# A mixture-of-experts backbone on one core: weights laid out in blocks by the host, two experts given 64 float32 slots in place of 128 split ones, and another order of the experts

## The chip, the core and the metric

The kernel runs on one core of one Trainium2 chip. The metric is the device time of one execution in microseconds (us), lower is better. Engines are named as the profile names them: PE is the tensor engine (PEld its loads of stationary operands), DVE the vector engine, ACT the scalar engine, POOL the general-purpose engine, SP the engine whose queue issues the loads of weights.

## What is computed

The reference is a two-layer backbone over 256 latent and 256 context tokens of width 1024, in float32. Each layer has a token mixer (attention, retention and pooling heads between one input and one output projection), then a channel mixer: dense SwiGLU in the first layer, the two best of eight expert SwiGLUs in the second. Norms are modulated by a conditioning vector through a large matrix `w_mod`. The part that matters here is the last:

```python
def moe_swiglu(h, router, w1, w3, w2):
    logits = (h @ router).astype(jnp.float32)
    top_vals, top_idx = lax.top_k(logits, TOP_K)
    top_w = jax.nn.softmax(top_vals, axis=-1)
    gates = jnp.sum(jax.nn.one_hot(top_idx, N_EXPERTS, dtype=jnp.float32) * top_w[..., None], axis=-2)
    out = jnp.zeros_like(h)
    for e in range(N_EXPERTS):
        out = out + gates[..., e:e + 1].astype(h.dtype) * swiglu(h, w1[e], w3[e], w2[e])
    return out
```

256 tokens with two experts each make 512 places for eight experts. With the inputs that are timed the experts 0 to 7 get 15, 154, 50, 25, 52, 46, 80 and 90 tokens. Each expert has three matrices of 1024 by 2816 (or 2816 by 1024) float32 numbers, 33 MiB in all, so the eight hold 264 MiB.

## The kernel before

The program is one straight line of instructions for each engine; only the order in which the expert weights are fetched, and a loop at the very end, depend on the data. Weights come through SP's queue in loads of 1 MiB, one `[128, 2048]` float32 tile each (`wload`), into a ring of buffers that is used in turn. In the expert part the ring has 13 buffers (4 of `ring`, 3 of `ring2`, 6 of `ring3`), and one early load goes to memory that is lent (`LENT`). A load is issued when the reader of the load 13 places earlier is done with its buffer, and SP issues loads in order.

Before the change the weight matrices lie in DRAM as the reference has them. A block of rows and columns is picked by the load's pattern, so each partition's 2048 numbers come in pieces as wide as the block: 256 columns (1 KB), 512 (2 KB, `moe_w1` and `moe_w3`), 1024 (4 KB, `moe_w2`), or all 2048 (8 KB, most of `w_mod`).

**Experts** (`experts`). Expert 0 runs first, its address being known at once. The seven others follow by falling load; place 1 is the fullest of them. `SLOTS` has the number of token slots of each place and `RUNS` the order of the places, a pair in one bracket being worked chunk by chunk together. Tokens that find no slot go through the loop at the end. A place of 160 slots is a group of 128 and one of 32. For each place:

- `gather` picks the tokens of the slots by a product with a 0/1 matrix P and modulates them, on PE, then DVE and ACT.
- `up` makes the products with w1 and w3 for 512 features at a time, in five chunks and a half one: 22 loads.
- `act` makes silu(h1) * h3 and turns it by PE transposes (L1251).
- `down` makes the product with w2: 11 loads.
- `combine` weighs the result by the gates (ys, on ACT and then DVE), sends it back to the tokens by 8 products (L1352), and adds it to the sums `macc`.

A group of 128 slots works with split operands: each half load of weights (a unit of 1024 numbers a partition) is split by `wsplit` into a high part `wh` on ACT (L155) and a low part `wl` on DVE (L156), and PE makes three products for each pair of operands (`mm3`, L231 to L233). The pairs wh, wl live in `hl` buffers, four of each in the expert part. A group of 64 or 32 slots uses the float32 weights straight from the ring, in column tiles that work side by side (L1284 up, L1315 down); ACT and DVE have nothing to split for it. Its gathered tokens and its activations are in a tile `few64` (or `few32`), of which there was one.

```python
if m < 128:
    c = max(128, n * m // 128)
    for k in range(k0, k0 + nk):
        for j in range(n // c):
            nc.tensor.matmul(h[i][m * j:m * j + m, :c], lhsT=x[0][:, k],
                             rhs=t[:, k - k0, j * c:j * c + c], start=k == 0, stop=k == KB - 1,
                             tile_position=(0, m * j))
    continue
```

The tokens of the next run are gathered between the chunks of the one that runs (`ready`). Order on each engine follows the program, so what stands behind a waiting instruction on the same engine waits too. `hold` keeps the splits of the first expert's weights behind the routing.

Of the kernel before, what the change touches and what calls it, by code (L numbers as in the profile page):

```python
# [20 lines left out]
D = 1024  # L21
KB = 8
# [7 lines left out]
# One token tile is 128 rows; tiles 0, 1 hold the latent stream, tiles 2, 3 the context.  # L30
# Slots that an expert has in the order in which the experts run: expert 0 runs first, the others
# follow by falling load. What doesn't fit goes through the loop at the end.
SLOTS = (128, 160, 128, 128, 128, 64, 64, 64)
# Which of them run together, chunk by chunk.
RUNS = ((0,), (2,), (3,), (4,), (7,), (1, 6), (5,))
SCRATCH = 4096              # bytes a partition for the descriptors of Pool's DMAs
# [4 lines left out]
# Memory that the experts need late holds some of their first blocks of weights.  # L41
LENT = {11: "few64"}
# [4 lines left out]
def shape_constants():  # L47
    """Tables that follow from the shapes alone."""
# [32 lines left out]
def weave(main, side, ratio):  # L81
    """The steps of main, with `ratio` steps of side after each."""
    due = 0.0
    for _ in main:
        due += ratio
        while due >= 1:
            due -= 1
            next(side, None)


class Net:
# [61 lines left out]
    def split(self, hi, lo, x):  # L153
        """hi + lo == x exactly, each of them a float32r."""
# [3 lines left out]
    def wload(self, src, a, n):  # L158
        """A [128, a, n] block of weights (a * n == 2048) on its way from DRAM."""
        tag = self.lent.pop(0) if self.lent else None  # L160
        if tag:
            t = self.work.tile([128, 2048], F32, name="w", tag=tag, bufs=MA if tag == "acts" else 1)
        else:
            r = self.rings[self.turn % len(self.rings)]
            self.turn += 1
            t = r.tile([128, 2048], F32, name="w", tag="w")
        v = t.rearrange("p (a n) -> p a n", a=a)
        self.nc.sync.dma_start(v, src)
        return v
# [13 lines left out]
    def block(self, src, n, k):  # L183
        """Rows of src from block k on, 2048 elements a partition."""
        a = 2048 // n
        return self.wload(src[k * 128:(k + a) * 128].rearrange("(a p) n -> p a n", p=128), a, n)
# [16 lines left out]
    def product(self, units, outs, op, tail):  # L203
        """op for all units and outputs; the last `tail` units go output by output."""
# [23 lines left out]
    def mm3(self, out, a, b, start, stop):  # L228
        """out += a.T @ b of split operands."""
# [5 lines left out]
    def spin(self, p, n, w):  # L235
        """Products that nobody needs. They keep the PE at its full clock while it waits."""
# [4 lines left out]
    def setup(self):  # L241
# [29 lines left out]
        # silu of both conditioning vectors, as stationary columns  # L271
# [12 lines left out]
        # norm gains and pool scales by feature  # L284
# [14 lines left out]
    def decays(self):  # L299
        """log_sigmoid of the decay logits, on every partition: [layer, direction, head]."""  # L300
# [30 lines left out]
    def mod_group(self, l, g, ms=(), split=0):  # L331
        """2048 columns of c @ w_mod + b_mod, in steps of 128 rows of w_mod: row 32 j + m of the result holds
        512 of them (m: stream, context). In the first `split` steps VectorE weighs the rows for each m of ms
        and sums them by partition, and the tensor engine only sums the partitions."""
# [18 lines left out]
        for k in range(KB):  # L353
            w = self.wload(I["w_mod"][l, k * 128:(k + 1) * 128, g * 2048:(g + 1) * 2048]
                           .rearrange("p (a n) -> p a n", a=1), 1, 2048)
# [53 lines left out]
    def fill(self, n=1):  # L409
        """The next n steps of the modulation that is still to be done."""  # L410
# [3 lines left out]
    def gate_tile(self, l, g, m):  # L414
        """gate * norm_post on every partition."""
# [1212 lines left out]
```

## Time and profile before

| | |
|---|---|
| time of three runs | 1592.82 us median (1589.38 to 1595.25) |
| span of the profiled execution | 1588.2 us; no other time of that one execution is listed, and the three runs lie 1.2 to 7.1 us above its span |
| busy share PE, DVE, ACT, POOL | 97%, 63%, 48%, 2% |
| moved by DMA | 400.09 MB, 252 GB/s in the mean |
| expert part | from the first expert's first product at 806.18 us to the end |

Times are microseconds from the start of the span. A row of the timeline has the start, the length, engine, source line, operation, tiles and the number of instructions merged in it; in square brackets the idle time before it and who ended that. A busy PE is not a PE at its peak, because overlapping products all count as busy; how fast it works is read from the distance between the starts of its products.

### The profile page before, as it was taken

The page shows a single profiled execution, that of the slowest core. Times are in us where ns is not written, and L with a number is a line of the kernel's source. Part 1 is how long each engine was busy: PE and PEld are TensorE (multiplying, and loading weights), DVE is VectorE, ACT ScalarE, POOL GpSimd, SP SyncE. Part 2 cuts the span into 40 slices and gives each one's busy share as a digit, 9 for nine tenths or more (in the row PEclk, how much of TensorE's full clock was granted, in tenths as well). Part 3 has the DMA queues.
Part 4 walks back from the last instruction along what each step waited for, and adds up shares of the span by engine and source line. Part 5 has one row for each costly group of instructions (what it writes and reads, how often), then busy time and mean ns, then how long its engine had stood idle before and what let it go on. Part 6 is the DMA issues. An engine that isn't in the chain of part 4 may idle for free. (4 is left out here: it accounts for less than half of the span.)

```text
span 1588.2 us, 23352 instructions
## 1 busy us (share of the span) xinstructions
PE 1545.9 (97%) x9104; PEld 1167.4 (74%) x9105; DVE 1008.1 (63%) x1712; ACT 761.9 (48%) x1134; POOL 34.1 (2%) x69
## 2 busy tenths in 40 slices
PE   7999999999999999999999999999999999999996
PEld 5776668888888888786678788888887657674562
DVE  3596678764455456886789899999984144443411
ACT  4436644423213223567568878778773133333211
POOL 1010200000000010000000000000000000000000
PEclk9999999999999999999999999999999999999998
DMA  9873313344355533633588999999999999998994
GB/s 313 296 288 106 135 58 117 117 165 161 127 196 189 186 120 107 215 107 133 199 293 326 359 327 344 355 351 355 325 355 327 396 386 382 333 347 309 336 369 169
DMA packets 185574, 400.09 MB, mean 252 GB/s; under 512 B 9060, under 2 KB 60968, under 8 KB 180336
## 3 DMA queue, kind: packets, MB, share of 16 engines
q1 hardware_dynamic: 180432, 392.19, 69.6%
q0 software_dynamic: 2624, 5.54, 1.1%
q8 instruction: 73, 1.20, 0.3%
q10 hardware_dynamic: 2400, 0.79, 0.2%
q14 instruction: 45, 0.37, 0.1%
HBM read 397.41 MB, written 1.08 MB: 251 GB/s over the span
## 5 line engine op out<-in xcount | busy, mean ns | idle before, releaser
L155 ACT ACTIVATE wh<-w 128x1024 fp32r<-128x1024 f32 x442 | 462.0, 1061 | 361.7 <-PE at L233 108.9
L156 DVE TENSOR_TENSOR wl<-w,wh 128x1024 fp32r<-128x1024 f32 x442 | 531.5, 1222 | 158.1 <-ACT wh L155 146.1
L1284 PE MATMUL mm<-w,few 128*64 128x256 f32 (+2 forms) x1856 | 151.1, 335 | 0.0
L1284 PEld LDWEIGHTS mm<-w,few 128*64 128x64 f32 (+1 forms) x1856 | 99.3, 128 | 45.6 <-issue 11.7
L231 PE MATMUL mm<-hh,wh 128*128 128x512 f32 (+1 forms) x256 | 95.7, 374 | 1.2 <-ACT hh L155 1.2
L232 PE MATMUL mm<-hl,wh 128*128 128x512 f32 (+1 forms) x256 | 95.6, 374 | 0.0
L233 PE MATMUL mm<-hh,wl 128*128 128x512 f32 (+1 forms) x256 | 95.3, 372 | 0.0
L231 PE MATMUL mm<-wh,xh 128*128 128x512 f32 (+1 forms) x240 | 93.0, 387 | 0.6 <-ACT xh L155 0.6
L231 PE MATMUL at<-wh,xh 128*128 128x512 f32 (+1 forms) x240 | 90.8, 378 | 0.0
L232 PE MATMUL mm<-wl,xh 128*128 128x512 f32 (+1 forms) x240 | 89.9, 375 | 0.0
L233 PE MATMUL mm<-wh,xl 128*128 128x512 f32 (+1 forms) x240 | 89.7, 374 | 0.0
L232 PE MATMUL at<-wl,xh 128*128 128x512 f32 (+1 forms) x240 | 89.4, 373 | 0.0
L233 PE MATMUL at<-wh,xl 128*128 128x512 f32 (+1 forms) x240 | 89.1, 371 | 0.0
L233 PE MATMUL mm<-wh,hl 128*128 128x256 f32 (+1 forms) x240 | 80.6, 341 | 0.0
L361 DVE SCALAR_TENSOR_TENSOR wsum<-w,sc,wsum 128x1024 f32<-128x1024 f32 x48 | 59.6, 1280 | 30.3 <-DMA w<-in_w_mod_dram 30.3
L1315 PE MATMUL mm<-w,few 128*64 128x512 f32 (+1 forms) x352 | 77.1, 599 | 0.0
L232 PE MATMUL mm<-wl,hh 128*128 128x256 f32 (+1 forms) x224 | 75.3, 339 | 1.8 <-DVE wl L156 1.8
L231 PE MATMUL mm<-wh,hh 128*128 128x256 f32 (+1 forms) x224 | 74.9, 339 | 0.0
L232 PE MATMUL at<-hl,wh 128*128 128x512 f32 (+1 forms) x192 | 71.3, 371 | 0.0
L233 PE MATMUL at<-hh,wl 128*128 128x512 f32 (+1 forms) x192 | 71.3, 371 | 0.0
L231 PE MATMUL at<-hh,wh 128*128 128x512 f32 (+1 forms) x192 | 71.2, 371 | 0.0
L1247 ACT ACTIVATE mg<-mm 128x512 f32<-128x512 f32 (+3 forms) x54 | 24.8, 459 | 68.6 <-PE mm L1284 65.7
(459 smaller groups left out, 2860.6 us busy)
## 6 DMA issues: line engine op xcount, KB each, us to landing
w<-in_moe_w_dram SPq DMA_DIRECT2D x264, 1024.0 KB, 7.1
w<-in_w_mod_dram SPq DMA_DIRECT2D x48, 1024.0 KB, 5.2
w<-in_ffn_w_dram SPq DMA_DIRECT2D x33, 1024.0 KB, 5.5
w<-in_w_in_dram SPq DMA_DIRECT2D x16, 1024.0 KB, 5.2
w<-in_w_out_dram SPq DMA_DIRECT2D x8, 1024.0 KB, 5.2
gate<-gscr POOLq DMA_DIRECT2D x5, 512.0 KB, 4.8
band<-in_band_dram SPq DMA_DIRECT2D x4, 512.0 KB, 7.7
xin<-in_x_dram SPq DMA_DIRECT2D x2, 512.0 KB, 4.0
```

Source lines behind the costliest of these rows:

```text
L155: self.nc.scalar.activation(hi, x, AF.Copy)
L156: self.nc.vector.tensor_sub(lo, x, hi.bitcast(F32))
L231: mm(out, lhsT=a[0], rhs=b[0], start=start, stop=False)
L232: mm(out, lhsT=a[0], rhs=b[1], start=False, stop=False)
L233: mm(out, lhsT=a[1], rhs=b[0], start=False, stop=stop)
L361: nc.vector.scalar_tensor_tensor(x, y, c, x, op0=OP.mult, op1=OP.add)
L1247: nc.scalar.activation(s1[:r, :c], h1[:r, :c], AF.Silu)
L1284: nc.tensor.matmul(h[i][m * j:m * j + m, :c], lhsT=x[0][:, k], rhs=t[:, k - k0, j * c:j * c + c], start=k == 0, stop=k == KB - 1, tile_pos ...
L1315: nc.tensor.matmul(y[0][r:r + m], lhsT=x[0][:, b], rhs=w[:, j, c], start=f + j < a, stop=f + j >= FB - a, tile_position=(0, r))
```

## The change

1. **Layout.** `packed` and `blocks` cut every weight matrix on the host into the blocks that are loaded, so that a load is one contiguous MiB with 8 KB for each partition. `wload` takes that block; its callers give block numbers in place of slices. What lands in SBUF is the same.
2. **Slots.** Place 0 (expert 0) and place 4 (the fourth by load of the others) get 64 slots in place of 128.
3. **Order.** Places run as 0, 2, 4, 3, 5, (1, 6), 7 in place of 0, 2, 3, 4, 7, (1, 6), 5: groups of 64 and of 128 slots alternate.
4. **Memory.** There are two `few64` tiles in place of one, three pairs of `hl` buffers in the expert part in place of four, and no lent memory.

All else of the diff takes comments away, which moves line numbers by some 8 to 15.

```diff
-SLOTS = (128, 160, 128, 128, 128, 64, 64, 64)
-# Which of them run together, chunk by chunk.
-RUNS = ((0,), (2,), (3,), (4,), (7,), (1, 6), (5,))
+SLOTS = (64, 160, 128, 128, 64, 64, 64, 64)
+
+RUNS = ((0,), (2,), (4,), (3,), (5,), (1, 6), (7,))
...
-LENT = {11: "few64"}
...
     def wload(self, src, a, n):
-        tag = self.lent.pop(0) if self.lent else None
-        if tag:
-            t = self.work.tile([128, 2048], F32, name="w", tag=tag, bufs=MA if tag == "acts" else 1)
-        else:
-            r = self.rings[self.turn % len(self.rings)]
-            self.turn += 1
-            t = r.tile([128, 2048], F32, name="w", tag="w")
-        v = t.rearrange("p (a n) -> p a n", a=a)
-        self.nc.sync.dma_start(v, src)
-        return v
+        r = self.rings[self.turn % len(self.rings)]
+        self.turn += 1
+        t = r.tile([128, 2048], F32, name="w", tag="w")
+        self.nc.sync.dma_start(t, src)
+        return t.rearrange("p (a n) -> p a n", a=a)
...
-                c = D * (1 - i) + 256 * q
-                w = self.wload(self.I["w_mod"][0, :, c:c + 256].rearrange("(a p) n -> p a n", p=128), KB, 256)
+                w = self.wload(self.I["w_mod"][0, 0, 2 * q + i], KB, 256)
...
-                few = pool.tile([128, 4, 8 * n], F32, name="few", tag=f"few{n}", bufs=1)
+                few = pool.tile([128, 4, 8 * n], F32, name="few", tag=f"few{n}", bufs=1 + n // 64)
...
-                return a[e] if static else a[bass.ds(e, 1)].rearrange("o k n -> (o k) n")
+                return a[e] if static else a[bass.ds(e, 1)].rearrange("o b p n -> (o b) p n")
             w1, w3, w2 = at_("moe_w1"), at_("moe_w3"), at_("moe_w2")
-            return w1, w3, lambda f: w2[f * 128:(f + 2) * 128].rearrange("(a p) n -> p a n", p=128)
+            return w1, w3, lambda f: w2[f // 2]
...
         a = 2048 // n
         for k in range(0, KB, a):
-            t = self.wload(w[k * 128:(k + a) * 128, c0:c0 + n].rearrange("(a p) n -> p a n", p=128), a, n)
+            t = self.wload(w[c0 // 256 + k // a], a, n)
...
-            pools(es, ps=1, hl=4, work=1)
+            pools(es, ps=1, hl=3, work=1)
...
+def blocks(w, *widths):
+    out, c = [], 0
+    for n in widths:
+        a = 2048 // n
+        x = w[..., c:c + n].reshape(*w.shape[:-2], -1, a, 128, n)
+        out.append(np.moveaxis(x, -3, -2).reshape(*w.shape[:-2], -1, 128, 2048))
+        c += n
+    return np.concatenate(out, -3)
...
+    if name in ("moe_w1", "moe_w3"):
+        return blocks(a, *[512] * 5, 256)
...
+    if name in ("moe_w2", "ffn_w2"):
+        return blocks(a, 1024)
```

Three places show what the change moves. First PE, at the end of the first expert and the start of the second. `mm<-w,few` are products of a 64-slot group with weights from the ring, `at<-ys,GT` those of `combine`, `mm<-wh,xh` the first of the second expert, which has 128 slots. Before:

```order
L231 MATMUL mm<-wh,xh 128x512
L232 MATMUL mm<-wl,xh 128x512
L1352 MATMUL at<-ys,GT 128x512
L233 MATMUL mm<-wh,xl 128x512
L1352 MATMUL at<-ys,GT 128x512 x2
L1352 MATMUL at<-ys,GT 128x512 x3
```

And now:

```order
L1314 MATMUL at<-cst,G 128x128 x2
L1316 MATMUL at<-gatep,G 128x1 x2
L1302 MATMUL mm<-w,few 64x512 x40
L1339 MATMUL at<-ys,GT 128x512 x8
L223 MATMUL mm<-wh,xh 128x512
L224 MATMUL mm<-wl,xh 128x512
```

Before, the combining products of the first expert stood in between products of the second; now all eight stand in one piece ahead of the second's first.

Next ACT at the same place; `wh<-w` are splits of weights, here those of the second expert around the first's `ys`. Before:

```order
L155 ACTIVATE wh<-w 128x1024 x22
L1331 ACTIVATE GT<-at 128x256
L155 ACTIVATE wh<-w 128x1024
L1344 ACTIVATE ys<-mm,gcol 128x512
L1344 ACTIVATE ys<-at,gcol 128x512
L1355 ACTIVATE macc<-at 128x512 x4
```

And now:

```order
L1234 ACTIVATE mg<-mm 128x128
L1247 ACTIVATE few<-at 128x128
L1318 ACTIVATE GT<-at 128x256
L1331 ACTIVATE ys<-mm,gcol 128x512
L1342 ACTIVATE macc<-at 128x512 x4
L153 ACTIVATE wh<-w 128x1024 x6
```

Before, splits went on up to `ys` and beyond; now there are none for a 64-slot expert, and the first split for the second expert stands behind the first expert's `ys` and the four copies into `macc`.

Last DVE, where the third run ends (place 4, with 64 slots now; place 3 is next). `wl<-w,wh` are the low parts of splits. Before (where the second run ends, the row of order that has the same neighbours):

```order
L156 TENSOR_TENSOR wl<-w,wh 128x1024
L1333 COPY gcol<-at 128x1
L1345 SCALAR_TENSOR_TENSOR ys<-mm,gcol,ys 128x512
L1345 SCALAR_TENSOR_TENSOR ys<-at,gcol,ys 128x512
L1357 TENSOR_TENSOR macc<-macc,at 128x512 x4
L156 TENSOR_TENSOR wl<-w,wh 128x1024 x5
```

And now:

```order
L1194 TENSOR_SCALAR G<-cst,rankp 128x128 x2
L1320 COPY gcol<-at 128x1
L1332 SCALAR_TENSOR_TENSOR ys<-mm,gcol,ys 128x512
L1344 TENSOR_TENSOR macc<-macc,at 128x512 x4
L154 TENSOR_TENSOR wl<-w,wh 128x1024 x10
L1235 TENSOR_TENSOR mg<-mg,at 128x512
```

On DVE too the first low part for the next expert now stands behind `ys` and the four sums into `macc`, with no split ahead of them.

## Rows read from the trace of the kernel before

**Rows 1.** The page, part 2: DMA's busy tenths in 40 equal slices.

```profile
DMA  9873313344355533633588999999999999998994
```

**Rows 2.** Stretches: busy us of each engine, granted clock, DMA share, GB/s.

```profile
906.00:1006.00 100.00, 100.00 (x489) 83.22 (x488) 90.36 (x92) 79.99 (x92) 0.00 (x0) 1.00 0.97 346
1286.00:1288.00 2.00, 2.00 (x31) 1.47 (x33) 2.00 (x4) 2.00 (x3) 0.00 (x0) 0.51 1.04 386
```

**Rows 3.** PE timeline: starts of experts, a gather, and the first combining products.

```profile
806.18 0.50 PE L231 MATMUL mm<-wh,xh 128*128 128x512 f32 x1 [0.62 <-ACT xh L155]
...
830.03 3.73 PE L1226 MATMUL at<-P,res 128*128 128x128 f32 x32
...
909.01 0.51 PE L1352 MATMUL at<-ys,GT 128*128 128x512 f32 x1
...
1009.07 0.50 PE L1352 MATMUL at<-ys,GT 128*128 128x512 f32 x1
...
1206.47 0.65 PE L1284 MATMUL mm<-w,few 128*64 128x256 f32 x2
```

**Rows 4.** What SP's queue waited for, 800 us to the end: total us, times, longest.

```profile
SPq L168 <- DVE wl L156: 282.7, 118, 6.3
```

**Rows 5.** DMA packets in 10:20, 1300:1340, 1243:1263 and 75:85 us.

```profile
DMA packets 3154, 3.58 MB, mean 358 GB/s; under 512 B 185, under 2 KB 2633, under 8 KB 3154
...
DMA packets 7745, 15.43 MB, mean 386 GB/s; under 512 B 234, under 2 KB 234, under 8 KB 7741
...
DMA packets 2119, 8.18 MB, mean 409 GB/s; under 512 B 126, under 2 KB 126, under 8 KB 2118
...
DMA packets 664, 4.15 MB, mean 415 GB/s; under 512 B 64, under 2 KB 172, under 8 KB 172
```

**Rows 6.** PE timeline of a 64-slot expert (the last): chunks of 512 features, then down.

```profile
1515.98 7.13 PE L1284 MATMUL mm<-w,few 128*64 128x256 f32 x64
...
1523.41 7.13 PE L1284 MATMUL mm<-w,few 128*64 128x256 f32 x64
...
1545.71 1.97 PE L1284 MATMUL mm<-w,few 128*64 128x128 f32 x32
...
1549.13 1.10 PE L1338 MATMUL at<-macc,cst 128*128 128x512 f32 x2
```

**Rows 7.** Timeline of all engines where a 64-slot expert (place 7) hands over.

```profile
1263.37 19.10 PE L1315 MATMUL mm<-w,few 128*64 128x512 f32 x88
...
1282.58 1.29 ACT L1233 ACTIVATE few<-at,modc,modc 128x64 f32<-128x64 f32 x4 [18.72 <-PE mm L1315]
1283.75 0.70 ACT L1344 ACTIVATE ys<-mm,gcol 128x512 fp32r<-128x512 f32 x1
...
1284.51 1.52 PE L1352 MATMUL at<-ys,GT 64*128 64x512 f32 x8 [2.03 <-ACT ys L1344]
1285.83 2.48 DVE L1357 TENSOR_TENSOR macc<-macc,at 128x512 f32<-128x512 f32 x4 [0.59 <-PE at L1352]
...
1288.23 2.35 DVE L156 TENSOR_TENSOR wl<-w,wh 128x1024 fp32r<-128x1024 f32 x2
1289.87 0.50 PE L232 MATMUL mm<-wl,xh 128*128 128x512 f32 x1
```

**Rows 8.** Timeline of all engines inside a 128-slot expert (place 2).

```profile
944.84 0.39 PE L233 MATMUL at<-wh,xl 128*128 128x512 f32 x1
...
945.27 1.06 ACT L155 ACTIVATE wh<-w 128x1024 fp32r<-128x1024 f32 x1 [0.30 <-PE at L233]
...
946.14 0.68 DVE L1248 TENSOR_TENSOR mg<-mg,at 128x512 f32<-128x512 f32 x1
946.20 0.39 PE L233 MATMUL mm<-wh,xl 128*128 128x512 f32 x1
```

**Rows 9.** PE timeline, start of the program: two waits.

```profile
17.30 1.07 PE L465 MATMUL md<-w,sc 128*32 128x256 f32 x16 [0.47 <-DMA w<-in_w_mod_dram]
...
49.87 0.50 PE L232 MATMUL mm<-wl,hh 128*128 128x512 f32 x1 [1.76 <-DVE wl L156]
```

More of the change, by code (lines that the diff above doesn't have):

```diff
@@ L183, in block @@
     def block(self, src, n, k):
-        a = 2048 // n
-        return self.wload(src[k * 128:(k + a) * 128].rearrange("(a p) n -> p a n", p=128), a, n)
+        return self.wload(src[k * n // 2048], 2048 // n, n)
     def units(self, src, n, back=False, pace=0, ahead=None, place=lambda k: None, order=None):
@@ L353, in mod_group @@
         for k in range(KB):
-            w = self.wload(I["w_mod"][l, k * 128:(k + 1) * 128, g * 2048:(g + 1) * 2048]
-                           .rearrange("p (a n) -> p a n", a=1), 1, 2048)
+            w = self.wload(I["w_mod"][l, g, k], 1, 2048)
             if k < split:
@@ L598, in op @@
                 self.mm3(o[:, :n], (hh[:, k, s], hl[:, k, s]), (wh, wl), start, stop)
-            yield from self.product(self.units(I["w_in"][l, :, cols:cols + n], n, pace=rate * 512 // n, ahead=ahead), out, op, tail)
+            yield from self.product(self.units(I["w_in"][l, cols // 256:(cols + n) // 256], n, pace=rate * 512 // n, ahead=ahead), out, op, tail)
             for t in tiles:
@@ L676, in mixer @@
             more, self.filler = self.filler, iter(())
-            ready = self.begin(xin, hh, hl, I["w_in"][l, :, 0:512])
+            ready = self.begin(xin, hh, hl, I["w_in"][l, 0:2])
             next(ready)
@@ L758, in op_qk @@
                 self.mm3(o[:, :n], (wh[:, s], wl[:, s]), (hh[:, k, :n], hl[:, k, :n]), start, stop)
-            yield from self.product(self.units(I["w_in"][l, :, 768:1280], 512, pace=rate), out, op_qk, 1)
+            yield from self.product(self.units(I["w_in"][l, 3:5], 512, pace=rate), out, op_qk, 1)
             qq, kk = self.features()
@@ L964, in mixer @@
         if need:
-            side = self.product(self.units(w[:, 0:512], 512, back=True, pace=1), outs, op_out, 1)
+            side = self.product(self.units(w[0:2], 512, back=True, pace=1), outs, op_out, 1)
         else:
@@ L972, in mixer @@
             outs.update(more)
-            u = self.units(w[:, 512:1024], 512, pace=1,
+            u = self.units(w[2:4], 512, pace=1,
                            place=lambda k: [sl([128, 1024], "wx", F32R) for _ in range(2)] if k >= 4 else None)
@@ L1076, in dense @@
             for b0 in range(0, nb, 2):
-                cols = slice((fb + b0) * 128, (fb + b0) * 128 + 256)
-                w1 = self.wload(I["ffn_w1"][:, cols].rearrange("(a p) n -> p a n", p=128), KB, 256)
-                w3 = self.wload(I["ffn_w3"][:, cols].rearrange("(a p) n -> p a n", p=128), KB, 256)
+                w1, w3 = (self.wload(I[x][(fb + b0) // 2], KB, 256) for x in ("ffn_w1", "ffn_w3"))
                 split = lambda b: [self.wsplit(w[:, :, b * 128:b * 128 + 128]) for w in (w1, w3)]
@@ L1114, in dense @@
             for k0 in range(0, nb, 2):
-                r0 = (fb + k0) * 128
-                w = self.wload(I["ffn_w2"][r0:r0 + 256].rearrange("(a p) n -> p a n", p=128), 2, D)
+                w = self.wload(I["ffn_w2"][(fb + k0) // 2], 2, D)
                 held += [(k0 + j, self.wsplit(w[:, j:j + 1])) for j in range(2)]
@@ L1140, in dense @@
         self.fh = hh, hl = self.features()
-        self.ahead = self.block(I["w_in"][1, :, 512:768], 256, 0)
+        self.ahead = self.block(I["w_in"][1, 2:3], 256, 0)
         for m in (1, 0):
@@ L1496, in experts @@
             cur = nxt
-        outs = pool.tile([128, 4, 512], F32, name="outs", tag="few64", bufs=1)
+        outs = pool.tile([128, 4, 512], F32, name="outs", tag="few64", bufs=2)
         outs = [outs[:, i] for i in range(4)]
@@ L1544, in run @@
             self.ring = es.enter_context(tc.tile_pool(name="ring", bufs=4))
-            self.rings, self.turn, self.lent = [self.ring], 0, []
+            self.rings, self.turn = [self.ring], 0
             self.scr = es.enter_context(tc.tile_pool(name="scr", bufs=1, space=DRAM))
@@ L1592, in run @@
             self.rings, self.turn = self.rings[n:] + self.rings[:n] + [more] * RING3, 0
-            self.lent = [LENT.get(i) for i in range(max(LENT) + 1)]
             self.experts(self.work)
@@ L1600, with packed @@
         "moe_router", "moe_w1", "moe_w3", "moe_w2")
+def blocks(w, *widths):
[6 more added lines that the diff above has]
+    return np.concatenate(out, -3)
+def packed(name, a):
+    if name == "w_in":
+        return blocks(a, 512, 256, 512, 256, 512)
+    if name == "w_out":
+        return np.stack([blocks(a[0], 512, 512), blocks(a[1], 1024)])
+    if name == "w_mod":
+        first = blocks(a[0, :, :2 * D], *[256] * 8).reshape(2, 4, 128, 2048)[::-1].swapaxes(0, 1).reshape(8, 128, 2048)
+        rest = blocks(a, 2048, 2048, 2048).reshape(2, 3, 8, 128, 2048)
+        return np.stack([np.stack([first, *rest[0, 1:]]), rest[1]])
+    if name in ("moe_w1", "moe_w3"):
+        return blocks(a, *[512] * 5, 256)
+    if name in ("ffn_w1", "ffn_w3"):
+        return blocks(a, *[256] * 11)
+    if name in ("moe_w2", "ffn_w2"):
+        return blocks(a, 1024)
+    return a
 def host_arrays(inputs):
@@ L1608, in host_arrays @@
             a = a.reshape(a.shape[1:])
-        arrays[name] = np.ascontiguousarray(a)
+        arrays[name] = np.ascontiguousarray(packed(name, a))
     arrays["cst"], arrays["dist"], arrays["band"] = shape_constants()
```

## The prediction

> **What bounds the kernel now.** I read the page first, then the clock and the shares by stretch, then the timelines of PE where experts begin and end. PE is busy 97% of 1588.2 us, but a busy PE says little, so I looked at distances. In the expert part the products of a 128-slot expert follow each other without a gap: in [rows 8] from the L233 at 944.84 to the one at 946.20 lie six products, 0.227 us each, and the granted clock of 906:1006 is 1.00 [rows 2]. That PE is what sets the pace is seen one level up: the first combining products of three experts in a row start at 909.01, 1009.07 and one equal step later [rows 3], 100.06 us for one whole 128-slot expert, its gather of 3.73 included [rows 3].
>
> The second thing that could set the pace is the load of weights, since an expert is 33 MiB whatever its slots. The DMA share in the last half of the page is 8 to 9 tenths [rows 1], and 0.97 in 906:1006 [rows 2]. But the queue was held back there: it waited 282.7 us in 118 waits for DVE's low parts [rows 4], that is for a ring buffer to be read, and packets in flight share the engines, so their time counts as busy also when nothing is short. Rates tell more: 358 GB/s where the pieces are 1 KB, 386 for 2 KB, 409 for 4 KB, 415 for 8 KB [rows 5]. One MiB thus takes 2.93, 2.72, 2.56 and 2.53 us.
>
> **The two experts.** Place 0 has 15 tokens and place 4 has 52, by the counts of the reference; both fit in 64 slots, and the loop at the end gets nothing. Each such expert now works as the last one does. A chunk there takes 1523.41 - 1515.98 = 7.43 us, the half chunk with what follows it 1549.13 - 1545.71 = 3.4 [rows 6], down 19.10 [rows 7]. With the gather of 3.73 [rows 3] that is 5 x 7.43 + 3.4 + 19.1 + 3.7 = 63.4 us.
>
> **Their seams.** What a 64-slot expert costs beyond that is seen where place 7 gives way to a 128-slot place [rows 7]. Down ends at 1263.37 + 19.10 = 1282.47. Then ACT and DVE each weigh a half of the result, PE combines (1284.51, 1.52 long), DVE adds to `macc` until 1288.31, and only then comes the first low part of the next expert's split, so that the first L232 starts at 1289.87: 7.4 us behind down. The order shown above has the same chain at both new seams: no split ahead of `ys` or `macc`. PE filled part of this gap with products of the 32-slot group; at the new seams there is no such group and it waits, but the chain through DVE sets the end either way. One piece is gone: ACT first wrote `few` for the place after (1282.58, 1.29 long), which had waited 18.72 us for down to free the only `few64`, and `ys` stood behind it. With two tiles that write is done earlier, which saves 1283.75 - 1282.58 = 1.2. The new seam is 6.2 us, the expert 63.4 + 6.2 = 69.6 us, and the gain 100.1 - 69.6 = 30.5 each: **-61.0** for two. The old seam in front of (1, 6) is kept, with place 5 there, and loses the same stall: **-1.2**.
>
> **The clock at the seams.** In 1286:1288 the granted clock is 0.51, the lower level (1.2 GHz), after PE had waited 2.03 us for `ys` [rows 2, 7]. Two us at half the clock lose 1 us of work. At the new seams PE waits longer, and what is lost may fall on the next products, which the 6.2 don't hold; part falls in the wait and is free. I take 0.85 for each, **+1.7**, with 0 and 2 x 1.7 as ends, the upper one if the low clock lasts through 3.4 us of products.
>
> **Three pairs of split operands.** A unit of weights occupies PE for six products, 1.36 us [rows 8]. With three pairs the next split into a pair may start when its products end, and must be done two units and one product later, 2 x 1.36 + 0.23 = 2.95. The loop is ACT 1.06 behind its release (0.04 after it in the row) [rows 8], then DVE's low part, 2.35 / 2 = 1.18 [rows 7], with a handover: 2.36. That leaves 0.5 us. It is broken when a gather's work falls in between, DVE's `mg` of 0.68 [rows 8] and ACT's like: some 0.8 us at most for each chunk, 5.5 chunks and two of the lone 128-slot experts, 9 us if every one is hit. With four pairs one unit more, 1.36, covers it. Most such work falls where the splits are ahead, so I take **+2**, with 0 and +9 as ends.
>
> **The layout and the loads.** With loads of 8 KB pieces I take 2.53 us each [rows 5]. Whether PE is starved is a ledger: 33 loads an expert, at most 13 ahead. The stages are 70 us (place 0), 98, 72, 98 and 78 (place 5 with what is beside it). A stage of 70 brings 70 / 2.53 = 27.7 of its 33, so the lead falls from 13 to 7.7; 98 us bring 38.7, and it is back at 13; then 72 leaves 8.5, 98 gives 13, 78 leaves 10.8.  By the old mean of 2.67 us for w1, w3 and w2 the leads are 6.2, 9.9, 3.9, 7.6 and 3.8: no stall either. So in the expert part the layout is worth **0**; what hides it is PE's work on 128-slot experts. The pair (1, 6) and the last expert ask for no more than before.
>
> At the program's start loads do limit. PE waited 0.47 us for one of `w_mod` [rows 9], which nine such loads repeat at most (4.2 us), and 1.76 for the first split [rows 9]; against that, most of `w_mod` came in pieces of 8 KB already. I take **-1.5**, between 0 and -6.
>
> **The first expert.** At 806.18 PE had waited 0.62 us for the split of its gathered tokens [rows 3]; a 64-slot expert has no such split: **-0.7** with its handover, between 0 and that.
>
> **Sum.** -61.0 - 1.2 - 1.5 - 0.7 + 2 + 1.7 = -60.7. From the profiled execution's 1588.2 this gives a span of 1527.5; the median lies 4.6 above that span, and with that kept the time is **1532 us**. `LENT` is costed at nothing: it held one load early, in front of an expert that begins with 13 in the ring; without it one load of 2.53 is later, and the first lead of 7.7 becomes 6.7.
>
> **Rivals.** *Loads become the bound.* The ledger rests on 2.53, measured over 10 us in `w_mod`. At 358 GB/s, the row of the 1 KB pieces, a load takes 2.93 us: 70 us bring 23.9, the lead falls to 3.9, 98 us take it only to 4.3, 72 leave it 4.1 loads short (12 us of stall), 98 bring 0.4 more than they use, and 78 leave it 6 short (17.6 us). Some 30 us come back: 1562. For it speaks the share of 0.97 at 346 GB/s [rows 2]; against it 386, 409 and 415 [rows 5], all above 358 and in stretches where a queue had something to do. I give 0.08. The Trainium skill states in "DMA: Bandwidth & Descriptors", section "Specifications", a limit of HBM for each core of about 358 GB/s. By that rule the time would be the 1562 of this rival; the trace does not agree, since three of its four stretches lie above the figure, up to 415.
>
> *Slower than before.* If contiguous loads land slower than the pieces did, because each of them touches fewer parts of memory at once, the gain goes altogether. By the same ledger the sum of the five stages is 416 us and 165 loads less a first lead of 13 are to be brought, so that 61 us of stall need (416 + 61) / 152 = 3.13 us a load, 335 GB/s. Below that rate the kernel is slower than 1592. For it: the 346 GB/s of a stretch that is 0.97 busy [rows 2]. Against it: 8 KB pieces were the fastest of the rows [rows 5]. 0.03.
>
> *The seams cost nothing*, because gathers of the next place or splits with room in the three pairs fill them: two seams of 6.2 and their clock, about 14 us, would go, 1518. The order speaks against it. 0.07. *The slots don't do it:* a count that does not fit sends an expert's tokens through the loop, a whole fetch of 33 loads more (33 x 2.53 = 83 us), 1615; the counts exclude it but for a mistake of mine, 0.01.
>
> **How the numbers follow.** The forecast has 0.81. Its own range takes the ends of the terms: hl from 0 to 9, clock 0 to 3.4, start 0 to -6: about 1524 to 1543. To hold 8 in 10 it must take in what the ledger leaves open, so I go to 1518 below (no seams) and 1556 above, most of the way to the load-bound case. A difference of 0.5%, 8 us, is about what a measurement of this kernel can tell from no change. The far end of the load rival, as its rate nears 335 GB/s, and the near end of the second lie within 0.5% of no change, 0.01 of each: same 0.02. The rest of the second rival and the overflow are slower, 0.03; all else is faster, 0.95.
>
> **What would show it.** In the changed trace: place 0 from its first product to its first combining one about 66 us, where a 128-slot expert had 100; chunks of 7.4 at both new places, and above 8 only if loads stall; PE's wait between the combining products and the next L231 about 4 us at two seams; no ACT wait of 18 us for down at `few`; waits of PE or ACT for a DMA near zero from 800 us on (if they sum to 10 or more, the load rival holds); rates of about 400 GB/s while a 64-slot expert runs; no wait of more than a few tenths of PE for `wl` inside a 128-slot expert (if there are many, hl cost more than 2). The forecast is wrong if place 4 or 5 waits for weights.

## The result, and the profile after

The changed kernel takes 1537.88 us (median of 4 runs, 1536.6 to 1538.84), the kernel before 1591.1 in the same comparison (4 runs, 1589.01 to 1595.25): a ratio of 0.9667, with a 95% interval from 0.9651 to 0.9682. That is 53 us less. The forecast was 1532, its range 1518 to 1556. The profiled execution has a span of 1534.8 us where 1527.5 was forecast, so 53.4 us came of the 60.7 that the sum had, and 7.3 are missing. They are the interesting part, for several terms were wrong and partly cancel. In the medians 5.9 us are missing (1537.88 against 1532), since the median now lies 3.1 us above the profiled span and not 4.6.

The page's part 2 of the changed kernel, 40 slices, answers to [rows 1]; ahead of it stands the line of PE before the change:

```profile
PE   7999999999999999999999999999999999999996
...
PE   7999999999999999999999899998999999999996
DMA  8773323353454433532359999899998998988893
GB/s 345 296 285 112 117 78 110 110 193 136 138 206 160 170 146 143 173 133 92 142 219 399 420 419 362 345 420 420 415 364 340 406 420 320 359 335 306 329 410 136
```

PE has two slices of 8 in the expert part where it had 9 before; those are the hand-overs. DMA now moves up to 420 GB/s in whole slices. Is PE short of weights? The waits of PE in the expert part, from 800 us on (who waited for whom, us in total, times, longest):

```profile
PE mm L224 <- DVE wl L154: 5.4, 3, 3.1
PE at L1339 <- ACT ys L1331: 3.2, 4, 0.8
PE mm L223 <- ACT wh L153: 2.9, 1, 2.9
PE at L1238 <- DVE mg L1235: 2.1, 3, 0.7
```

No DMA is among them, and the waits for `wl` and `wh` are those of the three hand-overs. SP's queue, of which [rows 4] shows the largest wait in total before, is still held by readers of the ring, now above all by products of groups with 64 or 32 slots:

```profile
SPq L161 <- PE mm L1271: 237.8, 104, 24.1
SPq L161 <- DVE wl L154: 178.3, 70, 6.4
...
SPq L161 <- DMA w<-in_moe_w_dram: 24.9, 16, 2.0
```

In 16 waits, 24.9 us in all, the queue was held by a load itself; none of them reached PE. So the load case, the first rival, did not come. Four stretches (us, busy us of PE, PEld, DVE, ACT and POOL, granted clock, DMA share, GB/s; they answer to [rows 2]) show the rest:

```profile
850.00:870.00 20.00, 20.00 (x93) 6.85 (x93) 0.57 (x3) 0.66 (x2) 0.00 (x0) 1.00 1.01 420
876.00:880.00 4.00, 3.47 (x9) 2.83 (x10) 2.75 (x3) 2.04 (x3) 0.00 (x0) 0.57 1.01 420
906.00:945.00 39.00, 38.94 (x195) 31.43 (x194) 35.23 (x34) 31.80 (x36) 0.00 (x0) 1.00 0.99 395
1053.00:1057.00 4.00, 4.00 (x11) 3.14 (x10) 2.59 (x3) 1.06 (x1) 0.00 (x0) 0.51 1.01 420
```

While place 0 ends (850:870) loads run at 420 GB/s, 2.50 us for a MiB. The Trainium skill, "DMA: Bandwidth & Descriptors", section "Specifications", has about 358 GB/s as the limit for a core; the trace disagrees. It fits what the Trainium skill says in "Perfetto Trace Analysis", section "Roofline", that a core which is active alone can pull more than its share, up to about 435 GB/s of its 16 DMA engines. In 876:880 and 1053:1057, right behind two hand-overs, PE worked at half its clock.

PE's timeline, with the lines that answer to [rows 3], from place 0 to place 5:

```profile
803.92 9.71 PE L1271 MATMUL mm<-w,few 128*64 128x256 f32 x86
813.57 0.44 PE L1238 MATMUL at<-cst,mg 128*128 128x128 f32 x2
...
824.84 7.13 PE L1271 MATMUL mm<-w,few 128*64 128x256 f32 x64
...
852.72 17.39 PE L1302 MATMUL mm<-w,few 128*64 128x512 f32 x80
...
977.86 0.65 PE L1271 MATMUL mm<-w,few 128*64 128x256 f32 x2
...
1027.46 19.10 PE L1302 MATMUL mm<-w,few 128*64 128x512 f32 x88
...
1052.35 0.80 PE L224 MATMUL mm<-wl,xh 128*128 128x512 f32 x1 [3.05 <-DVE wl L154]
...
1154.45 0.65 PE L1271 MATMUL mm<-w,few 128*64 128x256 f32 x2
```

Four places (0, 2, 4, 3) run from 803.92 to 1154.45, 350.5 us; before, the four places ahead of place 7 ran from 806.18 to 1206.47 [rows 3], 400.3. The gain there is 49.8 us, where the sum had 57.3 (61.0 less 2 less 1.7). The expert part begins 2.3 us earlier (2.2 forecast, which is luck, as is shown below), and from 1154.45 to the end it is 380.35 against 381.7 from 1206.47 on, 1.4 less (1.2 forecast). So all that is missing lies in those four places. The first hand-over, all engines, answers to [rows 7]:

```profile
870.15 0.69 ACT L1331 ACTIVATE ys<-mm,gcol 128x512 fp32r<-128x512 f32 x1 [16.94 <-PE mm L1302]
...
870.89 1.52 PE L1339 MATMUL at<-ys,GT 64*128 64x512 f32 x8 [0.79 <-ACT ys L1331]
872.21 2.06 ACT L1342 ACTIVATE macc<-at 128x512 f32<-128x512 f32 x4 [1.37 <-PE at L1339]
874.14 2.97 ACT L153 ACTIVATE wh<-w 128x1024 fp32r<-128x1024 f32 x3
875.25 3.50 DVE L154 TENSOR_TENSOR wl<-w,wh 128x1024 fp32r<-128x1024 f32 x3 [3.62 <-ACT wh L153]
875.27 0.49 PE L223 MATMUL mm<-wh,xh 128*128 128x512 f32 x1 [2.86 <-ACT wh L153]
876.53 0.80 PE L224 MATMUL mm<-wl,xh 128*128 128x512 f32 x1 [0.77 <-DVE wl L154]
877.12 0.63 PE L225 MATMUL mm<-wh,xl 128*128 128x512 f32 x1
877.55 0.63 PE L223 MATMUL mm<-wh,xh 128*128 128x512 f32 x1
```

Down ends at 852.72 + 17.39 = 870.11 and the first L224 starts at 876.53: 6.4 us, and 1052.35 - 1046.56 = 5.8 at the second, against 6.2 forecast. ACT's four copies into `macc` stand ahead of its first split, PE waits 2.86 us for that split, and then products start every 0.425 us, at the half clock, until 879.6 (behind the second hand-over until 1057.1).

One thing no row of before had announced: inside the up phase of place 2 the products of 512 columns are further apart.

```profile
890.21 0.40 PE L225 MATMUL mm<-wh,xl 128*128 128x512 f32 x1
...
891.61 0.40 PE L225 MATMUL mm<-wh,xl 128*128 128x512 f32 x1
```

Six products take 1.40 us, 0.233 each, where it was 1.36 and 0.227 [rows 8].

### The profile page after: what moved, and what is told of

Its sections match the earlier page's. It is cut to its first block, busy times and chain, and to the rows that moved or that the text cites. A ratio compares the mean times of both kernels' runs of the same rounds, so it can differ in the third digit from the quotient of the medians.

```text
span 1534.8 us, 23054 instructions
## 1 busy us (share of the span) xinstructions
PE 1483.9 (97%) x9186; PEld 1077.8 (70%) x9187; DVE 843.9 (55%) x1562; ACT 621.9 (41%) x996; POOL 34.2 (2%) x69
## 4 chain that ended last, share of the span: by engine, by line
PE 89%; DVE 6%; ACT 3%; DMA 1%; issue 1%; ACTq 0%; DVEq 0%
PE mm L1271 15%; PE mm L224 11%; PE mm L223 11%; PE mm L225 10%; PE mm L1302 7%; PE at L223 7%; PE at L224 7%; PE at L225 7%; PE at L1213 2%; PE md L358 1%; PE at L732 1%; PE at L709 1%; PE at L1238 1%; DVE wl L154 1%; PE at L720 1%; PE at L906 1%
## 5 line engine op out<-in xcount | busy, mean ns | idle before, releaser
L154 DVE TENSOR_TENSOR wl<-w,wh 128x1024 fp32r<-128x1024 f32 x310 | 374.1, 1223 | 198.1 <-ACT wh L153 189.0
L153 ACT ACTIVATE wh<-w 128x1024 fp32r<-128x1024 f32 x310 | 323.9, 1060 | 366.6 <-PE at L225 114.3
L1271 PE MATMUL mm<-w,few 128*64 128x256 f32 (+2 forms) x2624 | 229.3, 340 | 0.0
L1271 PEld LDWEIGHTS mm<-w,few 128*64 128x64 f32 (+1 forms) x2624 | 150.4, 129 | 69.2 <-issue 14.4
L1302 PE MATMUL mm<-w,few 128*64 128x512 f32 (+1 forms) x528 | 116.6, 598 | 0.0
L224 PE MATMUL mm<-hl,wh 128*128 128x512 f32 (+1 forms) x256 | 95.7, 374 | 0.0
L1235 DVE TENSOR_TENSOR mg<-mg,mm 128x256 f32<-128x256 f32 (+2 forms) x36 | 13.6, 378 | 131.8 <-ACT mg L1234 131.8
L1302 PEld LDWEIGHTS mm<-w,few 128*64 128x64 f32 (+1 forms) x528 | 32.7, 132 | 70.2 <-issue 69.7
L224 PE MATMUL mm<-wl,hh 128*128 128x256 f32 (+1 forms) x224 | 74.7, 336 | 1.8 <-DVE wl L154 1.8
L224 PE MATMUL at<-hl,wh 128*128 128x512 f32 (+1 forms) x192 | 71.3, 371 | 0.0
L1234 ACT ACTIVATE mg<-mm 128x256 f32<-128x256 f32 (+3 forms) x54 | 22.8, 422 | 112.9 <-PE mm L1271 108.8
L224 PE MATMUL mm<-wl,xh 128*128 128x512 f32 (+1 forms) x144 | 56.8, 394 | 5.6 <-DVE wl L154 5.4
L223 PE MATMUL mm<-wh,xh 128*128 128x512 f32 (+1 forms) x144 | 57.3, 398 | 2.9 <-ACT wh L153 2.9
L223 PEld LDWEIGHTS mm<-hh,wh 128*128 128x128 f32 x256 | 48.2, 188 | 11.2 <-issue 2.1
```

The lines of the kernel that those rows point to most:

```text
L153: self.nc.scalar.activation(hi, x, AF.Copy)
L154: self.nc.vector.tensor_sub(lo, x, hi.bitcast(F32))
L223: mm(out, lhsT=a[0], rhs=b[0], start=start, stop=False)
L224: mm(out, lhsT=a[0], rhs=b[1], start=False, stop=False)
L1234: nc.scalar.activation(s1[:r, :c], h1[:r, :c], AF.Silu)
L1302: nc.tensor.matmul(y[0][r:r + m], lhsT=x[0][:, b], rhs=w[:, j, c], start=f + j < a, stop=f + j >= FB - a, tile_position=(0, r))
```

## The experiments

Each time is the median of the kernel's runs; the ratio is to the kernel before on the same chip, with its interval. The rows come from four comparisons, in which the kernel before took 1591.1, 1590.56, 1590.8 and 1589.7 us, so that 2 or 3 us between two rows are better read from the traces.

| kernel | us | ratio | 95% interval |
|---|---|---|---|
| the change | 1537.88 | 0.9667 | 0.9651 to 0.9682 |
| layout alone, on the kernel before | 1588.54 | 0.9984 | 0.9971 to 0.9997 |
| the change with the old layout | 1538.1 | 0.9672 | 0.9653 to 0.9691 |
| the change with the old order | 1533.45 | 0.9656 | 0.9631 to 0.9682 |
| 128- and 64-slot experts in pairs | 1569.85 | 0.988 | 0.9861 to 0.9899 |
| three pairs, on the kernel before | 1598.37 | 1.0053 | 1.0035 to 1.0072 |
| the change with four pairs, ring of 12 | 1537.48 | 0.9667 | 0.9642 to 0.9692 |
| seven useless products in the hand-overs | 1539.58 | 0.9683 | 0.9659 to 0.9707 |
| three of them | 1535.2 | 0.9651 | 0.963 to 0.9672 |
| first chunk ahead of the combining | 1528.16 | 0.9628 | 0.9589 to 0.9668 |
| `xh`, `xl` at lower bytes | 1534.99 | 0.965 | 0.9628 to 0.9672 |
| all stationary operands low, split weights high | 1539.18 | 0.9676 | 0.9653 to 0.9699 |
| that memory, first chunk ahead at two hand-overs | 1526.55 | 0.9592 | 0.9569 to 0.9615 |

**Layout alone.** The changed kernel's code with slots, order, `hl` and `LENT` of before:

```diff
-SLOTS = (64, 160, 128, 128, 64, 64, 64, 64)
+SLOTS = (128, 160, 128, 128, 128, 64, 64, 64)
-RUNS = ((0,), (2,), (4,), (3,), (5,), (1, 6), (7,))
+RUNS = ((0,), (2,), (3,), (4,), (7,), (1, 6), (5,))
```

> The kernel before with the weights laid out in blocks and nothing else. My theory: the layout saves about 1.5 us at the start and nothing in the expert part, since weights are ahead there. Open is why products of 512 columns started every 0.227 us in the up phases of before and every 0.233 after the change. If the contiguous loads do that, the up phases here show 0.233 and the time is about 1597 (four 128-slot experts at 1.65 us and the pair at 1.6, less 1.5); rival, that slots, order or the memory of three pairs do it: 0.227 here and about 1589.5. A second rival, that bandwidth is worth much: below 1580.

It came out at 1588.54, 2 us below the kernel before (0.5 to 4.6 by the interval), about the 1.5 expected, and the products in its up phases started every 0.227 us. So contiguous loads are not what spreads them. Where the 2 us lie is not shown: in the profiled execution the first expert begins at 806.00, where it began at 806.18 before.

**The change with the old layout.** The kernel before with the slots, the order, two `few64` and three pairs of the change, and nothing lent.

> The changed kernel with weights loaded from the old layout; slots, order, two few64 and three pairs as changed. My theory: leads of weights never run out (2.67 us a load by the rows of before, smallest lead about 7 of 13), so the time stays within 1534 to 1540: 1539.5 if the layout is worth its 1.5 us at the start alone, 1534.5 if the contiguous loads are also what slows the products to 0.233, which would then be 0.227 here. Rival: the layout carries the 64-slot experts; PE then waits for weights in places 0, 4, 5 or 7 and the time is 1550 or more.

1538.1: the layout is worth nothing here that these runs can tell. The rival fell, PE waited for no weights. Loads ran slower, though, as a stretch in place 0 shows, first of this kernel, then of the change:

```profile
811.00:870.00 59.00, 59.00 (x469) 34.28 (x467) 7.75 (x26) 7.33 (x19) 0.00 (x0) 1.00 1.04 393
...
811.00:870.00 59.00, 59.00 (x459) 33.29 (x455) 6.23 (x17) 7.33 (x19) 0.00 (x0) 1.00 1.01 419
```

**The change with the old order.** Only `RUNS` as before, so that places 4 and 7, 64 slots both, follow each other.

> The changed kernel with the order of the places of before (0, 2, 3, 4, 7, (1, 6), 5), so that two 64-slot experts follow each other. My theory: one hand-over from 64 to 128 slots less, and that costs 6 us and 2 us of low clock, so about 1530; the ledger of loads at 2.5 us gives leads of 7.5 and 4.9 after the two, no stall. Rival: alternation is what keeps PE fed; then PE waits for weights in place 7 and the time is 1538 or more.

1533.45, on the side of my theory (one hand-over less), but 4.4 us in place of 8, and the intervals overlap. Place 7 was not starved:

```profile
1152.00:1225.00 73.00, 72.13 (x585) 44.75 (x581) 11.63 (x33) 10.05 (x28) 0.00 (x0) 1.00 1.01 419
```

The alternation is thus not what feeds PE. Some of the other half is lost where places 2 and 3, both of 128 slots, now meet with three pairs. PE's timeline there, behind the first combining products of place 2 (977.46):

```profile
983.25 0.50 PE L224 MATMUL mm<-wl,xh 128*128 128x512 f32 x1 [1.94 <-DVE wl L154]
```

PE waits 1.94 us for a split. From combining to combining place 3 took 104.4 us (977.46 to 1081.87), where a 128-slot expert took 100.06 before; some 1.5 of that difference is the distance of its products.

**Pairs.** `RUNS = ((0,), (2, 4), (3, 5), (1, 6), (7,))`.

> The changed kernel with a 128-slot and a 64-slot expert worked together chunk by chunk: 0, (2, 4), (3, 5), (1, 6), 7. My theory: products of the 64-slot expert fill the wait for the splits, so two of the three hand-overs (6 us and 2 us of low clock each) go, and about 1522 comes out. Rival: a pair needs 66 loads in some 168 us, 2.54 us each, just what the loads take, and splits of two experts' chunks fall together; then stalls eat the gain and the time is 1535 to 1550.

A clear miss: 1569.85, worse than either case. Timeline of ACT and PE at the end of a chunk of place 4 beside place 2:

```profile
897.94 0.38 ACT L1234 ACTIVATE mg<-mm 128x256 f32<-128x256 f32 x1 [10.29 <-PE mm L1271]
898.22 2.94 ACT L153 ACTIVATE wh<-w 128x1024 fp32r<-128x1024 f32 x3
...
899.32 0.49 PE L223 MATMUL mm<-wh,xh 128*128 128x512 f32 x1 [1.43 <-ACT wh L153]
```

ACT takes the chunk's silu in program order, waits 10.29 us for the 64-slot products to end, and the splits of the next chunk stand behind it. PE then waits for a first split, chunk after chunk. It is the hand-over again, in small and many times. PE's waits for `wh` and `wl` sum to 24.1 us from 800 us on, 8.3 in the change; that is 16 of the 31 us by which the span is longer, and where the others lie was not taken apart.

**Three pairs on the kernel before, and four on the change.** One line each; the second also takes a ring buffer (`RING3` 5):

```diff
-            pools(es, ps=1, hl=4, work=1)
+            pools(es, ps=1, hl=3, work=1)
```

> The kernel before with three pairs of split operands in the expert part in place of four, nothing else. Two theories of the slower products (0.233 us a product in the up phases of the changed kernel, 0.227 before): if three pairs, or where in memory they and the tiles behind them then lie, make them slow, the up phases here show 0.233 and the time is about 7 us longer (1597); if slots or order do, 0.227 and 1590. My term for three pairs, waits of PE for split operands inside 128-slot experts, was 1 us for each of them: about 4 us of such waits here and 0 if the term was wrong.

> The changed kernel with four pairs, the memory taken from one ring buffer (12 in place of 13). If three pairs are behind the slower products, the up phases show 0.227 and the time is about 5 us shorter (1533); if not, 0.233 and 1538, for a ring of 12 leaves leads of 6 at the least.

The products stayed at 0.227 in the one and at 0.233 in the other: three pairs do not spread them. But the kernel before lost 7.6 us by them, while the changed one gains nothing from a fourth. One place of the loss, in the kernel before with three pairs, all engines, at the end of place 2:

```profile
1012.35 0.39 PE L231 MATMUL mm<-wh,xh 128*128 128x512 f32 x1
...
1012.55 1.06 ACT L155 ACTIVATE wh<-w 128x1024 fp32r<-128x1024 f32 x1 [0.99 <-PE mm L233]
1013.66 0.50 PE L231 MATMUL at<-wh,xh 128*128 128x512 f32 x1 [0.92 <-ACT wh L155]
```

PE waits 0.92 us for a split, right where one 128-slot expert hands over to the next and DVE and ACT also weigh and add up the result. An expert there took 102.1 us (combining starts at 1008.09 and 1110.17) in place of 100.06. In the change no 128-slot expert follows another, so that place doesn't exist. But it is only a part of the loss. Set beside those of the kernel before, product by product, the products fall behind by some 9 us in the expert part: about 1 at this meeting and 1 at the next, about 2 in the first chunk of place 0, about 1 in each of places 0, 2 and 3, mostly where down begins, and the rest behind place 4. Why the changed kernel, in which down begins and hand-overs come too, loses nothing by three pairs is not shown.

**Useless products in the wait.**

```diff
             cur = nxt
+            if i in (0, 2):
+                self.spin(self.at(), 7, 512)
```

> The changed kernel with seven products that nobody needs (512 columns of the constants, 0.49 us each at full clock) behind the combining products of places 0 and 4, in PE's wait for the next expert's first split. Theory: the clock falls because PE waits there; with the wait filled it stays at full level, the first products after the two hand-overs start every 0.23 us in place of 0.43, and 3.9 us are saved: about 1534. Rival: the clock falls there whatever PE does, or the filling delays the first product by as much: 1538 or more.

A miss of mine in size: each shows as two products of 0.45 us, so that seven took 6.28 us where the wait is 3, and the next product came late. Timeline of PE at the second hand-over:

```profile
1050.25 6.28 PE L230 MATMUL at<-cst 128*128 128x512 f32 x14 [0.55 <-DVE macc L1344]
1055.96 0.79 PE L223 MATMUL mm<-wh,xh 128*128 128x512 f32 x1
1056.60 0.39 PE L224 MATMUL mm<-wl,xh 128*128 128x512 f32 x1
1056.83 0.40 PE L225 MATMUL mm<-wh,xl 128*128 128x512 f32 x1
```

But the products behind it start every 0.23 us, so the clock did stay. With three in place of seven:

> The changed kernel with three useless products in place of the seven that were too many: each came as two passes, 6.3 us in all, where the wait is 2.9 and 3.5. Three fill 2.7 us. Theory that the clock fell by PE's wait and that this costs 3.9 us: no fall at the two hand-overs, first products every 0.23 us, about 1534. Rival: a shorter wait is still enough for a fall: 1537 to 1538.

1535.2, 2.7 less than the change in medians; the same stretch:

```profile
1053.00:1057.00 4.00, 4.00 (x19) 3.23 (x19) 3.47 (x4) 2.13 (x2) 0.00 (x0) 1.00 1.01 420
```

The clock is 1.00 where it was 0.51, with 19 products in place of 11. With the wait filled the clock stayed in both kernels, so the fall does come from PE's wait. The intervals of the times overlap; the gain is read from rows. From the first product of place 0 to that of place 5 it is 347.2 us (805.68 to 1152.87) in place of 350.5, 3.3 of the 3.9 expected.

**The first chunk ahead of the combining.** Behind places 0, 4 and 5 the next place's first step is written before `combine` (the rest of the edit, which puts the beginning of a place into a function `begin`, is left out here):

```diff
+            if i in (0, 2, 4):
+                started = begin(RUNS[i + 1], nxt)
+                started = *started[:2], chain([next(started[2])], started[2])
             for pos, ys in zip(run, yss):
                 for b, (n, y) in enumerate(zip(cur[pos][0], ys)):
```

> The changed kernel with the first chunk of the next place written ahead of the combining at the three hand-overs behind places 0, 4 and 5: the splits of the next expert then stand ahead of ys and macc on ACT and DVE, and the combining products between products of the next expert. Theory: a hand-over costs 6.4 and 5.8 us and the clock behind it 1.5 and 2.4, of which 1.9 for the combining products stay: 6 us saved at each of the first two, 2 at the third, where products of the 32-slot group fill the gap already: about 1523, and no clock fall. Rival: the splits find their weights or their pairs late and PE waits at the same places: 1536 or more.

1528.16, with one of the four runs at 1537.8. The first hand-over of this kernel, all engines, and the stretch around it (columns as in the four stretches above):

```profile
865.70 2.58 DVE L154 TENSOR_TENSOR wl<-w,wh 128x1024 fp32r<-128x1024 f32 x2
865.70 4.03 PE L1302 MATMUL mm<-w,few 128*64 128x512 f32 x16
865.96 1.06 ACT L153 ACTIVATE wh<-w 128x1024 fp32r<-128x1024 f32 x1 [0.49 <-DMA w<-in_moe_w_dram]
...
869.65 0.50 PE L223 MATMUL mm<-wh,xh 128*128 128x512 f32 x1
869.99 0.40 PE L224 MATMUL mm<-wl,xh 128*128 128x512 f32 x1
...
868.00:872.00 4.00, 4.00 (x18) 2.21 (x13) 0.28 (x1) 0.64 (x1) 0.00 (x0) 1.00 1.02 416
```

The splits are made while down runs and PE goes on without a gap or a fall of the clock. From the start of place 0 to the end of place 4 it is 236.3 us against 242.65, 6.4 less, and 5.1 less from there to the end of place 5; 6 each were forecast. From the end of place 5 to the end of the program it is 2.3 us longer, where 2 less was forecast; why, I did not find out.

**Where the operands lie.** Tiles lie in a pool in the order in which they are first asked for. First `xh` and `xl` alone are asked for early (the second line added); then `ma` too, and the pool of the split weights is opened last (the other two edits). Each edit also moves the tiles that come behind it:

```diff
         i8 = cst[:, C_I8:C_I8 + 8]
+        pool.tile([128, 4, 512], F32R, name="ma2", tag="acts", bufs=MA)
+        [pool.tile([128, KB, 128], F32R, name=i, tag=i, bufs=1) for i in ("xh", "xl")]
...
-            pools(es, ps=1, hl=3, work=1)
+            pools(es, ps=1, work=1, hl=3)
```

> The changed kernel with xh and xl, the stationary operands of the up products, asked for first, so that they lie at bytes 68672 to 76863 of a partition in place of 103808 to 111999; before the change they lay at 89664 to 97855, and ma, whose products started every 0.233 us in all kernels, at 105856 and up. Theory: where the stationary operand lies decides the distance of the products; then the up phases go back to 0.227, down stays at 0.233, and the time is 5 us shorter, about 1533. Rival: the order of the places or the 64-slot experts' loads do it: 0.233 and 1538 as before this edit.

> As the run before, with ma too at low bytes (44096 to 68671) and the split weights, the moving operands, up at 118240 to 142815. If the stationary operand's place alone counts, up and down both show 0.227, and the time is 8 us below the changed kernel's: 1530. If the moving operand's place counts as well, or instead, 0.233 stays in both and the time is 1538 or more.

PE's timeline with `xh` low, in the up phase of place 2, three products:

```profile
899.90 0.39 PE L225 MATMUL at<-wh,xl 128*128 128x512 f32 x1
...
900.58 0.40 PE L225 MATMUL at<-wh,xl 128*128 128x512 f32 x1
```

0.68 / 3 = 0.227, as before the change. Over all such products of this phase that follow each other directly the mean is 0.229, where it was 0.228 in the kernel before and 0.233 in the changed one. With the split weights high, six products:

```profile
883.88 0.39 PE L225 MATMUL mm<-wh,xl 128*128 128x512 f32 x1
...
885.29 0.40 PE L225 MATMUL at<-wh,xl 128*128 128x512 f32 x1
```

1.41 / 6 = 0.235; the mean over the phase is 0.234, in up and down alike. So for the products of up it is where the operands lie in the partition, and both count: 0.227 came only with both low, 0.233 to 0.235 when one was high. In time the edit to `xh` shows 2.9 us in medians and 3.8 in the spans, where 5 were expected. But 2.7 of the 3.8 lie ahead of the first expert, where `xh` has no part: it begins at 801.25 in place of 803.92. From there to the end it is 1.1 us less (729.8 against 730.9), and more than that is not shown to be the work of `xh`.

**Combined.** The memory of the last run, and the first chunk ahead for `i in (0, 2)` alone.

> The changed kernel with the memory of the run before and with the first chunk of the next place ahead of the combining behind places 0 and 4 alone (not behind 5, where it cost 2 us). If both gains hold and add: 1538 less 11 for the two hand-overs less 8 for the distance of products, about 1519. If the distance theory falls: 1526.

1526.55, the lowest time here, though not told apart from the 1528.16 (spans of 1526.0 and 1526.2). It is what was expected if the memory brings nothing, as it didn't. The edit to `xh` alone together with the first chunk ahead was not run.

## Why the prediction was right, and where it was wrong

**The bound.** PE sets the pace and weights are ahead of it: right. No wait of PE for a load from 800 us on, at 2.50 us a load, and none with the old layout either, as the ledger had it by both rates. The layout's price of 0 in the expert part holds. The 1.5 us at the start can't be read from where the first expert begins: that lay between 800.6 and 805.7 us in kernels of the new layout that have the same work ahead of it, and between 803.9 and 806.2 with the old. So the 2.3 us found there, against 2.2, are luck. Layout alone gave 2 us in medians, and no run shows where.

**The two experts**, the large term: the mechanism was right, the size not. I had 63.4 us for the body; the rows show 870.11 - 803.92 = 66.2 for place 0, and 1046.56 - 977.86 = 68.7 for place 4, of which 1.9 are place 2's combining products. The step that failed is "5 x 7.43". That spacing is the one from a chunk's transposes to the next chunk's, and the transposes of a chunk stand well into the next one (86 rows of products come ahead of the first pair, where a chunk has 64): the first pair starts at 813.57, 9.65 us behind the first product, and ends 0.4 later. A first chunk of 10.0 in place of 7.43 is about 2.6 us for each expert; the rest is work woven in. In all 2.8 + 3.4 = 6.2 us too little. The whole of place 7 would have given it: from 1206.47 to the end of its down at 1282.47 [rows 3, 7], 76.0 us, less 1.9 for the combining in it and less two gathers of 3.73, since it gathers for the three groups of the pair, about 66.6.

**The seams.** 6.4 and 5.8 against 6.2: right, and so the rival in which they cost nothing fell. But one round of combining products, 1.9 us, was in the seams and also in the 100.1 us of an expert behind a seam: counted twice, and so too pessimistic.

**The clock.** 1.7 forecast. Seven distances of 0.43 in place of 0.233 behind the first hand-over and eleven behind the second are 1.4 + 2.2 = 3.6, just above the upper end of 3.4. That it comes from PE's wait, the useless products showed.

**Three pairs.** 2 us forecast, 0 measured here and 7.6 on the kernel before. In the change PE waits for splits at the three hand-overs alone, so gathers do not break the loop as the term had it. In the kernel before, near the end of 9, the meetings of two 128-slot experts account for some 2 us, and the rest is not explained. (2.95 less 2.36 is 0.59 and not the 0.5 of the prediction; nothing hangs on it.)

**Not in the sum at all:** the distance of products, 0.006 us on the 240 up products of 512 columns of each of the two 128-slot experts, 2.9 us, and as much as 1.4 more in the pair.

Together in the four places: 6.2 - 1.9 - 0.2 + 1.9 - 2 + 2.9 = 6.9 of the 7.5 that are missing there. That the miss is small is in part luck: 11.0 us of errors one way met 4.1 the other way.

## What to carry to other kernels

Take the price of a stage from a whole stage in the trace, from its first product to the next one's, not from a spacing in its middle times a count: pipelined work fills at its start and drains at its end, and that was the largest error here. Where a stage that needs no preparation (no splits) is followed by one that does, look at what stands ahead of the first preparation in the queue of the engine that makes it; writing a chunk of it ahead of the last stage's closing work took 6.4 and 5.1 us from two hand-overs. The price of a spare buffer belongs to one order of stages: the fourth pair was worth 7.6 us in the kernel before and nothing in the changed one, so it has to be measured in the order that will run.

## What was not expected of the hardware

Bytes here are those at which the built programs place the tiles. Products of 512 columns start every 0.227 us when both operands lie low in a partition (`xh`, `xl` at bytes 68672 to 76863 or 89664 to 97855, split weights at 44096 to 76863) and every 0.232 to 0.235 when either lies higher (`xh` at 103808 and up, or split weights at 118240 and up). The down products had shown it before the change: their `ma`, at 105856 and up, went at 0.233. Where it turns (between 97855 and 103808 for the stationary operand, between 76863 and 118240 for the moving one), and why, stays open. Another rule would fit the runs as well at first sight: that the distance between the two operands decides, and not their height. It was not tried by a run of its own, but the rows speak against it. In the changed kernel `wl` lies 39232 to 47424 bytes below `xh`, and their products start every 0.233 us; in the kernel before `wh` lay 37376 to 49664 bytes below `xl`, and theirs started every 0.228 in the mean. The products of the 64-slot experts kept their 7.43 us a chunk whether `few` lay at 81472 or at 130432.

Loads of 8 KB pieces ran at 419 GB/s over 59 us of a 64-slot expert, in a stretch where the old layout gave 393.
